# A state-space layer whose matrix multiplications run in the order of the program text, with rows normed in three groups

## The chip, the cores and the metric

The kernel runs on one core of one Trainium2 chip. The metric is device time in microseconds (us) of one execution; the median of the runs is given. One profiled execution supplies the trace from which all rows below are read. The engines are TensorE (PE, with its weight loads as PEld), VectorE (DVE), ScalarE (ACT), GpSimd (POOL) and SyncE (SP), whose queue issues most DMA transfers. An engine runs its own instructions strictly in order and waits on semaphores for what the others produce.

## The reference, cut to what matters

The program is one inference step of a small decoder: an S5 state-space layer, a shared K/V projection, and a stick-breaking attention layer. The change touches only the state-space layer, up to its gelu:

```python
h = _rms_norm(x, g_pre)                  # x * rsqrt(mean(x*x) + eps) * g
uz = h @ w_in                            # 1024 -> 2048
u, z = uz[..., :SSM_WIDTH], uz[..., SSM_WIDTH:]
y, hr, hi = _s5_scan(u, ...)             # 64 groups of 16 channels, 64 complex states each
y = jax.nn.gelu(y)
y = y * jax.nn.sigmoid(y @ w_glu + b_glu)
y = y * jax.nn.silu(z)
return x + _rms_norm(y @ w_out, g_post), hr, hi
```

There are 1024 prompt rows and 8 x 8 sample rows, all in float32. The scan is a linear recurrence with a complex factor for each group and state; `y` is a projection of the states plus `d_skip * u`.

## The kernel before, in words

**Norm.** The prompt is read as eight tiles of 128 rows (tile t has the positions t, t+8, t+16, ...), and a ninth tile has the 64 sample rows. For each tile the loop at L230 to L264 loads `xt`, takes the sum of squares on ScalarE (L240), the reciprocal root on GpSimd (`rstd`, L70: a pow and some tiny steps), multiplies the rows by it and by the norm weights `gpre` on VectorE in one instruction (L243), transposes in eight blocks on TensorE (L249) into the PSUM banks `psa` and `psb`, and splits the transposed block into a high part `xh` (ScalarE) and the rest `xl` (VectorE, helper L205). Five buffers hold `xt`.

**Input gemms.** `xh` and `xl` are kept as three groups of columns (`ACH`): 3, 3 and 2 row tiles of 136 columns (128 chunks of the prompt and 8 samples), so 408, 408 and 272 columns. One gemm makes 128 output channels of u or z: for each group of columns, a *chunk*, 24 matmuls (8 slices of 1024, times three products of the split parts, L147 to L149), a copy out by ScalarE, and after the third chunk a store to `u_d` or `zs_d`. There are eight u gemms and eight z gemms. Their weights are split into `whi` (ScalarE) and `wlo` (VectorE, and GpSimd for the odd z gemms).

**Scan.** A loop over eight feature tiles `ft` (8 groups of channels each). The *matrices* of a tile: VectorE makes `wb`, `ep`, `tm`, `fk`, `tn` from parameters; TensorE transposes `ep` (`psm`, L342) into `et` and multiplies `fk` with `wb` (L355) into `kp`, which SP's queue spreads into `tg`. The factors `cs` are made on GpSimd (six instructions with a scratch `m`; on VectorE for the first tile) and spread by four transfers into `cf` (L386). There is one `cs` buffer. Then three *units* of 3, 3 and 2 groups: `ug` (u read back from `u_d`) times `et` gives the chunk states `psb` (L403); ScalarE copies the halves crosswise into `tb`, VectorE multiplies `psb` by `cf`, GpSimd multiplies `tb`, VectorE adds, VectorE scans (L418); again ScalarE makes `ts`, GpSimd and VectorE multiply, and VectorE's sum is `hs`. TensorE turns `ug` times `tg` plus `hs` times `fk` into `psa` (L435, L436), ScalarE applies gelu into `gt` (L437), and after three units `gt` is stored to `y_d` (L439). Behind the loop the eight tiles of `y_d` are loaded and split into `yh` and `yl` (L455 to L457) for the GLU gemm, `psmm<-yh,whi_g`, which follows the last z gemm.

**Order.** A scheduler sets the order of each engine's instructions by simulated times and by priority: the matrices and the units stand in `tc.high_priority(OFA)`, so the gemms are laid matmul by matmul where it expects TensorE to be free.

Of the kernel before, what the change touches and what calls it, by code (L numbers as in the profile page):

```python
# [10 lines left out]
F32 = mybir.dt.float32  # L11
# [34 lines left out]
LAG = 3  # L46
SHARE = (0.1, 0.2, 0.3, 0.4)
# [22 lines left out]
def rstd(nc, pool, ss, out, n, mul, tag, eng=None):  # L70

    E = eng or nc.vector
    v = pool.tile([128, n], F32, name=f"v_{tag}", tag="rs_v")
    r0 = pool.tile([128, n], F32, name=f"r0_{tag}", tag="rs_r")
    h = pool.tile([128, n], F32, name=f"h_{tag}", tag="rs_h")
    e = pool.tile([128, n], F32, name=f"e_{tag}", tag="rs_e")
# [124 lines left out]
def s5_layer(tc, nc, io, wp, bank, cst, gains, ident, sgn, zs_d, u_d, y_d, s2):  # L201
# [5 lines left out]
    with ExitStack() as sx:  # L207
# [21 lines left out]
        for t in (8, 0, 1, 2, 3, 4, 5, 6, 7):  # L229
            n = 128 if t < 8 else NTS  # L230
            xt = start.tile([128, D], F32, name=f"xt{t}", tag="xt", bufs=5)
            nc.sync.dma_start(xt[:n], xp[t] if t < 8 else io["x_sample"])
            if t == 8:
                nc.sync.dma_start(gpre, io["a_gpre"].to_broadcast([128, D]))
                nc.sync.dma_start(cst, io["consts"][:, 0:129])
            sq = start.tile([128, D], F32, name=f"sq{t}", tag="sq")
            ss = par.tile([128, 1], F32, name=f"ss{t}", tag="ss", bufs=2)
            if n < 128:
                V.memset(ss, 1024.0)
            nc.scalar.activation(sq[:n], xt[:n], AF.Square, accum_out=ss[:n])  # L240
            rt = par.tile([128, 1], F32, name=f"rt{t}", tag="rt", bufs=2)
            rstd(nc, par, ss, rt, 1, 1.0 / D, f"a{t}", Q)
            V.scalar_tensor_tensor(xt[:n], xt[:n], rt[:n], gpre[:n], op0=ALU.mult, op1=ALU.mult)  # L243
            for i in range(2):
                ps = bank("a" if i else "b")
                p3 = ps.rearrange("p (a b) -> p a b", a=4)[:, :, :n]
                for j in range(4):
                    k = 4 * i + j
                    nc.tensor.transpose(p3[:, j], xt[:n, k * 128 : (k + 1) * 128], ident[:n, :n])  # L249
                ks = slice(4 * i, 4 * i + 4)  # L250
                for c, (t0, m) in enumerate(ACH):
                    if t < 8:
# [24 lines left out]
        def gemm_u(ft, w=None):
            nc.sync.dma_start(u_d[ft], gemm("u", ft, lambda o, ps: nc.scalar.activation(o, ps, AF.Copy), w))  # L278

        def gemm_z(ft):  # L280
            nc.sync.dma_start(zs_d[ft], gemm("z", ft, lambda o, ps: nc.scalar.activation(o, ps, AF.Copy)))

        gemm_u(0, w_first)
        gemm_u(1)
# [21 lines left out]
        for i in range(2):  # L306
# [8 lines left out]
        units = 0  # L315

        for ft in range(KT):
            with tc.high_priority(OFA):
                gs = slice(ft * 8, ft * 8 + 8)

                pk = pk_all[:, gs, :]
                sb = tp.tile([128, 4, 8, GC], F32, name=f"sb{ft}", tag="sb", bufs=2)
                nc.scalar.dma_start(sb, io["s5_bc"][ft, :, 0:4])
                wb = tp.tile([128, 4, 8, GC], F32, name=f"wb{ft}", tag="wb")
                tt(V, wb[:, 0:2], sb[:, 0:2], bc(bc(wri[:, 0, gs], 2, GC), 1, 2), ALU.mult)
                tt(V, wb[:, 2:4], sb[:, 0:2][:, ::-1], bc(wri[:, 1:3, gs], 3, GC), ALU.mult)
                tt(V, wb[:, 0:2], wb[:, 0:2], wb[:, 2:4], ALU.add)
                V.tensor_scalar(sb[:, 2:4], sb[:, 2:4], sgn, None, op0=ALU.mult)

                ep = tp.tile([128, 8, L, GC], F32, name=f"ep{ft}", tag="ep")  # L330
                tm = tp.tile([128, 8, L, GC], F32, name=f"tm{ft}", tag="tm")
                lrv = pk[:, :, K_LR : K_LR + 8][:, :, ::-1]
                liv = pk[:, :, K_LI : K_LI + 8][:, :, ::-1]
                tt(V, ep, bc(lrv, 3, GC), bc(wb[:, 0], 2, L), ALU.mult)
                tt(V, tm, bc(liv, 3, GC), bc(wb[:, 1], 2, L), ALU.mult)
                tt(V, ep, ep, tm, ALU.subtract)
                et = tp.tile([128, 8, 128], F32, name=f"et{ft}", tag="et", bufs=2)
                for i in range(2):
                    ps = bank("m")
                    for j in range(4):  # L340
                        g = 4 * i + j
                        nc.tensor.transpose(ps[:, j * 128 : (j + 1) * 128], ep[:, g].rearrange("p a b -> p (a b)"), ident)  # L342
                    nc.scalar.activation(et[:, 4 * i : 4 * i + 4, :], ps.rearrange("p (a b) -> p a b", a=4), AF.Copy)
                fk = tp.tile([128, 8, L + 1, GC], F32, name=f"fk{ft}", tag="fk", bufs=2)
                tm2 = tp.tile([128, 8, L + 1, GC], F32, name=f"tn{ft}", tag="tm")
                tt(V, fk, bc(pk[:, :, K_LR : K_LR + 9], 3, GC), bc(sb[:, 2], 2, L + 1), ALU.mult)
                tt(V, tm2, bc(pk[:, :, K_LI : K_LI + 9], 3, GC), bc(sb[:, 3], 2, L + 1), ALU.mult)
                tt(V, fk, fk, tm2, ALU.subtract)
                tg = tgs[ft % 2]
                kp = tp.tile([16, 8, 128], F32, name=f"kp{ft}", tag="kp")  # L350
# [1049 lines left out]
```

## Time and profile before

| | |
|---|---|
| median of 3 runs | 1499.05 us (1498.17 to 1500.22) |
| profiled execution | 1500.17 us |
| span of its trace | 1498.4 us |
| TensorE busy | 1415.8 us (94%) |
| VectorE busy | 935.0 us (62%) |
| ScalarE busy | 718.2 us (48%) |
| GpSimd busy | 493.7 us (33%) |

Busy times are sums over the whole span; the state-space layer is its first 340 us. The profiled execution is 1.8 us longer than its span.

### The profile page before, as it was taken

What the parts mean: (1) busy time and instruction counts of PE and PEld (TensorE: products, weight loads), DVE (VectorE), ACT (ScalarE), POOL (GpSimd) and SP (SyncE); (2) the same over time, 40 slices, a digit from 0 to 9 for tenths busy, and PEclk for the clock granted to TensorE, in tenths of its full rate; (3) what the DMA queues carried; (4) which work ended last, traced back from release to release, by engine and by line L of the source; (5) the groups of instructions that cost most, each with busy time, mean ns of one, the idle gap of its engine ahead of it and who ended that gap; (6) DMA issues with size and microseconds to landing.
All of it is one profiled execution on the core that took longest, in us unless ns stands there. A gap on an engine that the chain in (4) does not pass through costs nothing.

```text
span 1498.4 us, 26819 instructions
## 1 busy us (share of the span) xinstructions
PE 1415.8 (94%) x9648; PEld 1145.8 (76%) x9648; DVE 935.0 (62%) x1506; ACT 718.2 (48%) x1424; POOL 493.7 (33%) x473
## 2 busy tenths in 40 slices
PE   4987988899999989999999999999998999998997
PEld 3987978899977889999988877666565665565766
DVE  6877887758755531110122149897888888789545
ACT  5233454454434433332333347676665766576321
POOL 6556565325412132222111012433323233334200
PEclk9999999999999999999999999999999999999999
DMA  5345556674134252232288755979878686754026
GB/s 197 103 129 139 140 126 163 145 251 145 58 106 132 91 224 91 85 123 100 103 314 298 255 201 192 339 284 326 295 257 289 250 308 219 268 190 139 11 82 213
DMA packets 129670, 276.41 MB, mean 184 GB/s; under 512 B 21633, under 2 KB 66562, under 8 KB 129538
## 3 DMA queue, kind: packets, MB, share of 16 engines
q1 hardware_dynamic: 127234, 268.41, 54.0%
q10 hardware_dynamic: 2304, 6.29, 1.3%
q8 instruction: 76, 1.25, 0.3%
q14 instruction: 56, 0.46, 0.1%
HBM read 224.55 MB, written 39.35 MB: 176 GB/s over the span
## 4 chain that ended last, share of the span: by engine, by line
PE 75%; DVE 9%; POOL 5%; DMA 4%; issue 3%; ACT 2%; SPq 1%; DVEq 0%; POOLq 0%; ACTq 0%
PE psmm L147 7%; PE psmm L149 7%; PE psmm L148 7%; PE psqk L147 6%; PE psqk L148 6%; PE psqk L149 6%; PE psa L949 5%; PE psb L1182 5%; PE psb L1164 4%; PE psa L990 4%; PE psqk L1139 3%; PE psqk L1140 2%; DMA cf<-cs 2%; PE psa L147 2%; PE psa L149 2%
## 5 line engine op out<-in xcount | busy, mean ns | idle before, releaser
L1120 POOL TENSOR_TENSOR ql<-q,qh 128x256 fp32r<-128x256 f32 x64 | 62.5, 977 | 285.6 <-ACT qh L1119 246.5
L1141 ACT ACTIVATE F<-psqk,bp 128x384 f32<-128x384 f32 (+2 forms) x192 | 111.3, 580 | 64.6 <-PE psqk L1140 49.2
L1146 DVE TENSOR_TENSOR_SCAN F<-F,maskb 128x256 f32<-128x256 f32 (+3 forms) x128 | 131.2, 1030 | 14.0 <-ACT F L1141 13.6
L1149 POOL TENSOR_TENSOR S<-S,F 128x255 f32<-128x255 f32 (+3 forms) x64 | 100.8, 1574 | 115.7 <-DVE F L1148 22.5
L1142 ACT ACTIVATE S<-psqk,bp 128x384 f32<-128x384 f32 (+2 forms) x192 | 111.4, 583 | 22.7 <-PE psb L1164 22.6
L1164 PE MATMUL psb<-cst,S 128*128 128x128 f32 x576 | 96.7, 285 | 4.4 <-DVE og L1186 3.8
L1164 PEld LDWEIGHTS psb<-cst,S 128*128 128x128 f32 x576 | 67.3, 143 | 35.1 <-issue 20.5
L1148 DVE TENSOR_TENSOR_SCAN F<-F 128x384 f32<-128x384 f32 (+1 forms) x64 | 78.9, 1233 | 20.4 <-ACT F L1141 19.8
L1182 PE MATMUL psb<-at,vr 128*64 128x256 f32 (+1 forms) x640 | 90.0, 369 | 1.2 <-DVE at L1168 1.2
L949 PE MATMUL psa<-vp,sat 128*32 128x256 f32 x1024 | 86.1, 388 | 0.1
L1139 PE MATMUL psqk<-ks,qh 128*128 128x384 f32 (+2 forms) x192 | 77.4, 404 | 6.9 <-DVE ks L1104 5.2
L990 PE MATMUL psa<-kp,qbd 128*32 128x256 f32 x1024 | 75.5, 389 | 0.5 <-PE psb L1164 0.5
L1182 PEld LDWEIGHTS psb<-at,vr 128*64 128x64 f32 x640 | 46.7, 137 | 36.6 <-issue 10.3
L1168 DVE TENSOR_TENSOR at<-psb,maskb 128x384 f32<-128x384 f32 (+3 forms) x128 | 60.3, 478 | 21.3 <-PE psb L1164 20.7
L147 PE MATMUL psmm<-xh,whi_u 128*128 128x408 f32 (+1 forms) x192 | 65.3, 341 | 3.7 <-ACT ut L278 3.1
L147 PE MATMUL psmm<-x,whi_g 128*128 128x408 f32 (+1 forms) x192 | 66.6, 347 | 1.1 <-DVE gt L739 1.1
L943 DVE TENSOR_TENSOR_SCAN sF<-sF 128x513 f32<-128x513 f32 x32 | 44.4, 1388 | 36.1 <-ACT sF L940 35.8
L1139 PEld LDWEIGHTS psqk<-ks,qh 128*128 128x128 f32 x192 | 37.0, 193 | 37.8 <-ACT S L1142 12.8
L1140 PE MATMUL psqk<-ks,ql 128*128 128x384 f32 (+2 forms) x192 | 65.8, 344 | 0.0
L148 PE MATMUL psmm<-xl,whi_u 128*128 128x408 f32 (+1 forms) x192 | 65.4, 341 | 0.0
L149 PE MATMUL psmm<-x,wlo_g 128*128 128x408 f32 (+1 forms) x192 | 64.9, 338 | 0.2 <-DVE wlo_g L141 0.2
L148 PE MATMUL psmm<-x,whi_g 128*128 128x408 f32 (+1 forms) x192 | 65.1, 339 | 0.0
(452 smaller groups left out, 4234.6 us busy)
## 6 DMA issues: line engine op xcount, KB each, us to landing
kp<-cache_kT SPq DMA_DIRECT2D x128, 512.0 KB, 6.0
vp<-cache_v SPq DMA_DIRECT2D x128, 512.0 KB, 5.7
cf<-cs SPq DMA_DIRECT2D x32, 256.0 KB, 5.4
q<-q_d SPq DMA_DIRECT2D x128, 64.0 KB, 4.6
u_d<-ut SPq DMA_DIRECT2D x8, 544.0 KB, 2.8
ug<-u_d SPq DMA_DIRECT2D x64, 68.0 KB, 2.9
y_d<-gt SPq DMA_DIRECT2D x64, 68.0 KB, 2.4
zs_d<-zt SPq DMA_DIRECT2D x8, 544.0 KB, 4.5
```

The lines of the kernel that those rows point to most:

```text
L147: nc.tensor.matmul(ps, sh, mh, start=(k == 0), stop=False)
L148: nc.tensor.matmul(ps, sh, ml, start=False, stop=False)
L149: nc.tensor.matmul(ps, sl, mh, start=False, stop=(k == n - 1))
L949: self.nc.tensor.matmul(po[32 * r : 32 * r + 32, 0:256], a[:, 32 * r : 32 * r + 32], rhs[:, r * 256 : (r + 1) * 256], start=start, stop=stop)
L990: nc.tensor.matmul(ps[32 * r : 32 * r + 32, half * 256 : half * 256 + 256], self.qbd[:, 2 * r + e, s, :], kt[:, :, 2 * r + e, :], start=(e ...
L1139: nc.tensor.matmul(ps[:, :m], qh[:, w], ks[:, c0 : c0 + m], start=True, stop=False)
L1141: nc.scalar.activation(F[:, c0 : c0 + m], ps[:, :m], AF.Sigmoid, bias=bp[:, 1, h : h + 1], scale=-0.125)
L1142: nc.scalar.activation(S[:, c0 : c0 + m], ps[:, :m], AF.Sigmoid, bias=bp[:, 0, h : h + 1], scale=0.125)
L1146: V.tensor_tensor_scan(fr, fr, self.maskb[:, 512 - m : 512][:, ::-1], 1.0, ALU.mult, ALU.max)
L1149: (Q if i % 2 else V).tensor_tensor(S[:, 0 : n - 1], S[:, 0 : n - 1], F[:, 1:n], op=ALU.mult)
L1164: nc.tensor.transpose(ps[:, j * 128 : (j + 1) * 128], S[:, (j0 + j) * 128 : (j0 + j + 1) * 128], self.ident)
L1182: nc.tensor.matmul(po[hs, o:256], self.vr[pi][:, j, hs], ats[hh][j // 4][:, j % 4, o:256], start=(j == 0), stop=(j == nj - 1))
```

## The change

1. The norm runs over three groups of row tiles (four, three and two). All nine `xt` have a buffer. The multiplication by `gpre` is a GpSimd instruction of its own, ahead of the reciprocal root; the root is computed for a whole group, with its tiny steps on VectorE (the pow stays on GpSimd), and VectorE then multiplies each tile by its column of `rt`.
2. From behind the norm until the scan's pools are closed, TensorE's order is that of the program text (`tc.manual_schedule`). The gemms become a generator, `fills`, that yields after each chunk; the text takes six chunks, then seven and one around the first tile's matrices, then one in each of 26 steps of the scan loop (one more for each of the first three tiles). Five are left behind the loop.
3. The outputs of a unit come two units later than its states (`ULAG`), with three `hs` tiles instead of two. `tb` and `ts` share three buffers instead of four.

The other engines are still ordered by the scheduler.

```diff
+ULAG = 2
+FILLS = "u1 u2 z0 u3 u4 z1 u5 z2 u6 z3 u7 z4 z5 z6 z7".split()
...
-        for t in (8, 0, 1, 2, 3, 4, 5, 6, 7):
-            xt = start.tile([128, D], F32, name=f"xt{t}", tag="xt", bufs=5)
...
-            rstd(nc, par, ss, rt, 1, 1.0 / D, f"a{t}", Q)
-            V.scalar_tensor_tensor(xt[:n], xt[:n], rt[:n], gpre[:n], op0=ALU.mult, op1=ALU.mult)
...
+        for group in ((8, 0, 1, 2), (3, 4, 5), (6, 7)):
...
+            for e, t in enumerate(group):
...
+                xt = start.tile([128, D], F32, name=f"xt{t}", tag="xt", bufs=9)
...
+                nc.scalar.activation(sq[:n], xt[:n], AF.Square, accum_out=ss[:n, e : e + 1])
+                tt(Q, xt[:n], xt[:n], gpre[:n], ALU.mult)
+            rstd(nc, start, ss, rt, len(group), 1.0 / D, f"a{group[0]}")
...
+            for e, t in enumerate(group):
...
+                V.tensor_scalar(xt[:n], xt[:n], rt[:n, e : e + 1], None, op0=ALU.mult)
...
-        gemm_u(0, w_first)
-        gemm_u(1)
+        fills = chain(gemm("u", 0, w_first), *(gemm(n[0], int(n[1])) for n in FILLS))
+        st.enter_context(tc.manual_schedule(engines={mybir.EngineType.PE}))
+
+        def fill(n):
+            for _ in range(n):
+                next(fills, None)
+
+        fill(6)
...
+        first = matrices(0)
+        fill(7)
+        ahead(first)
+        fill(1)
+        ahead(first)
+        nxt = None
+        for n in range(3 * KT + ULAG):
+            ft, j = divmod(n, 3)
+            if n < 3 * KT:
+                with tc.high_priority(OFA):
+                    states(ft, j)
+            if j == 1 and ft + 1 < KT:
+                nxt = matrices(ft + 1)
+            fill(1)
+            if n >= ULAG:
+                with tc.high_priority(OFA):
+                    outputs(*divmod(n - ULAG, 3))
+            if nxt and j:
+                if j == 2 and ft < 3:
+                    fill(1)
+                ahead(nxt)
+                nxt = nxt if j == 1 else None
...
-        for ft in range(5, 8):
-            gemm_z(ft)
+        for _ in fills:
+            pass
```

`matrices(ft)` has the old matrices in two parts, up to the transposes, and from `kp` to the loads of `ug`; `states` and `outputs` have the old unit up to `hs`, and from `psa` on; `ahead` runs the next part with high priority.

TensorE, around the first and second feature tile, before (in names a number behind the letters is the feature tile or buffer, as in `ep1`, `hs0`; the last number only keeps names apart):

```order
L148 MATMUL psmm66_1699<-xl2_94,whi_u5_1642 128x272
L149 MATMUL psmm66_1699<-xh2_91,wlo_u5_1643 128x272
L147 MATMUL psmm66_1699<-xh2_91,whi_u5_1642 128x272
L342 MATMUL psm38_1075<-cst_63,ep1_1063 128x128 x4
L403 MATMUL psb43_1220<-ug1_1210,et1_1068 128x136
L435 MATMUL psa32_976<-ug0_952,tg0_792 128x136
L436 MATMUL psa32_976<-hs0_788,fk0_823 128x136
```

The same engine now, at the second tile's transposes:

```order
L149 MATMUL psmm39_1121<-xh0_89,whi_u4_1116 128x408
L150 MATMUL psmm39_1121<-xl0_92,whi_u4_1116 128x408
L151 MATMUL psmm39_1121<-xh0_89,wlo_u4_1117 128x408
L354 MATMUL psm40_1160<-cst_63,ep1_1154 128x128 x4
L354 MATMUL psm41_1166<-cst_63,ep1_1154 128x128 x4
L416 MATMUL psb42_1177<-ug0_1034,et0_952 128x136 x2
L149 MATMUL psmm43_1197<-xh1_90,whi_u4_1116 128x408
```

Before, the outputs of tile 0 and the transposes of tile 1 cut into a chunk (`psmm66`); now both stand between whole chunks of 24 matmuls, and the chunk at tile 1's transposes is of `u4`, no longer of `u5`.

GpSimd at the first unit, before (`cs1` and `cs2` are the factors of tiles 1 and 2, `tb0_0` the first unit's copy, `ts0_0` its second):

```order
L205 TENSOR_TENSOR cs1_1111<-cs1_1111,m1_1112 128x512
L205 TENSOR_TENSOR m2_1370<-uu_569 128x512
L205 TENSOR_TENSOR tb0_0_966<-tb0_0_966,cf0_861 128x384
L205 TENSOR_TENSOR cs2_1369<-uu_569 128x512 x2
L205 TENSOR_TENSOR cs2_1369<-cs2_1369,m2_1370 128x512
L205 TENSOR_TENSOR ts0_0_977<-ts0_0_977,cf0_861 128x384
```

and now:

```order
L207 TENSOR_TENSOR cs1_1284<-cs1_1284,m1_1285 128x512
L207 TENSOR_TENSOR m2_1576<-uu_504 128x512
L207 TENSOR_TENSOR cs2_1575<-uu_504 128x512 x2
L207 TENSOR_TENSOR cs2_1575<-cs2_1575,m2_1576 128x512
L207 TENSOR_TENSOR m2_1576<-uu_504 128x512
L207 TENSOR_TENSOR dk1_1273<-cst_63,dcol_505 16x128
L207 TENSOR_TENSOR tb0_0_1047<-tb0_0_1047,cf0_1029 128x384
L207 TENSOR_TENSOR cs2_1575<-cs2_1575,m2_1576 128x512
L143 TENSOR_TENSOR wlo_z1_1331<-wraw_z1_1328,whi_z1_1330 128x1024
L207 TENSOR_TENSOR m3_1860<-uu_504 128x512
L207 TENSOR_TENSOR ts0_0_1057<-ts0_0_1057,cf0_1029 128x384
```

Most of `cs2` has moved ahead of the first unit's `tb0_0`, and a `wlo_z1` stands between `tb0_0` and `ts0_0`.

VectorE in the norm, now, at the third group (`rt6` is the group's root, `xl0` the first group of columns; `ex1_dt` and `ex3_dt` are parameter work):

```order
L254 TENSOR_SCALAR xt6_282<-xt6_282,rt6_280 128x1024
L254 TENSOR_SCALAR xt7_287<-xt7_287,rt6_280 128x1024
L102 SCALAR_TENSOR_TENSOR ex3_dt_519<-ex3_dt_519,ex2_dt_518 128x96
L207 TENSOR_TENSOR xl0_92<-psa8_198,xh0_89 128x4x128
L207 TENSOR_TENSOR xl1_93<-psb9_235,xh1_90 128x4x128
```

and before, at the same two tiles:

```order
L205 TENSOR_TENSOR xl1_93<-psb9_258,xh1_90 128x4x128
L205 TENSOR_TENSOR xl1_93<-psa10_265,xh1_90 128x4x128
L243 SCALAR_TENSOR_TENSOR xt6_336<-xt6_336,rt6_341,gpre_88 128x1024
L98 TENSOR_SCALAR ex3_dt_584<-ex2_dt_583 128x96
L102 TENSOR_SCALAR ex1_dt_582<-ex1_dt_582 128x96
L243 SCALAR_TENSOR_TENSOR xt7_368<-xt7_368,rt7_373,gpre_88 128x1024
L100 SCALAR_TENSOR_TENSOR ex3_dt_584<-ex3_dt_584,ex2_dt_583 128x96
```

Before, `xl1` of the fourth row tile was made ahead of the last tiles' multiplications; now the last block of `xl0`, of the third row tile, comes behind them.

## Rows read from the trace of the kernel before

**Rows 1.** Busy time (us, instructions) of engines by stretch; clock, DMA share, GB/s.

```profile
0.00:50.00 50.00, 27.03 (x146) 24.09 (x147) 34.13 (x82) 23.79 (x47) 24.35 (x74) 0.90 0.44 148
50.00:87.40 37.40, 35.92 (x218) 35.62 (x216) 33.54 (x85) 9.18 (x16) 25.54 (x26) 1.00 0.53 146
95.07:274.74 179.67, 152.39 (x1038) 144.25 (x1036) 140.87 (x231) 78.61 (x179) 109.61 (x85) 0.95 0.55 134
274.74:294.54 19.80, 18.53 (x136) 17.62 (x137) 14.52 (x33) 12.51 (x29) 5.43 (x6) 1.00 0.75 178
...
87.39:328.17 240.78, 212.23 (x1440) 203.11 (x1441) 176.24 (x298) 111.10 (x243) 129.00 (x101) 0.96 0.59 148
```

**Rows 2.** What TensorE waited for, 0 to 520 us: total, times, longest.

```profile
PE psb L249 <- DVE xt L243: 19.9, 5, 11.8
PE psa L435 <- ACT gt L437: 10.0, 4, 5.0
PE psa L436 <- DVE hs L205: 8.4, 4, 3.5
```

**Rows 3.** Timeline: start, duration, what, [idle before it <- releaser].

```profile
49.80 0.35 PE L147 MATMUL psmm<-xh,whi_u 128*128 128x408 f32 x1
...
87.39 0.66 PE L342 MATMUL psm<-cst,ep 128*128 128x128 f32 x4 [1.48 <-DVE ep L205]
...
95.07 0.57 DVE L205 TENSOR_TENSOR psb<-psb,cf 128x384 f32<-128x384 f32 x1 [2.07 <-ACT tb L411]
...
99.80 0.57 DVE L205 TENSOR_TENSOR psb<-psb,tb 128x384 f32<-128x384 f32 x1 [3.87 <-POOL tb L205]
...
274.74 0.57 DVE L205 TENSOR_TENSOR psb<-psb,cf 128x384 f32<-128x384 f32 x1 [0.58 <-ACT tb L411]
...
289.45 0.55 DVE L205 TENSOR_TENSOR hs<-psb,ts 128x381 f32<-128x381 f32 x1
...
294.54 0.57 DVE L205 TENSOR_TENSOR psb<-psb,cf 128x384 f32<-128x384 f32 x1 [0.29 <-ACT tb L411]
...
294.57 0.40 PE L435 MATMUL psa<-ug,tg 128*128 128x136 f32 x2
294.81 0.40 PE L436 MATMUL psa<-hs,fk 128*128 128x136 f32 x2
...
309.68 0.42 DVE L205 TENSOR_TENSOR hs<-psb,ts 128x254 f32<-128x254 f32 x1 [0.43 <-POOL ts L205]
...
328.17 0.35 PE L147 MATMUL psmm<-yh,whi_g 128*128 128x408 f32 x1
```

**Rows 4.** What VectorE waited for, 95.07 to 274.74 us.

```profile
DVE psb L205 <- ACT ts L426: 12.3, 13, 1.1
DVE psb L205 <- POOL tb L205: 8.0, 3, 3.9
DVE hs L205 <- POOL ts L205: 8.0, 5, 3.4
DVE psb L205 <- ACT tb L411: 6.8, 10, 2.1
DVE sb L328 <- DMA sb<-s_bc: 3.2, 2, 1.7
```

**Rows 5.** GpSimd by form, 0 to 340 us: busy us, mean ns | idle before.

```profile
L205 POOL TENSOR_TENSOR cs<-uu 128x512 f32<-128x512 f32 x14 | 19.3, 1396 | 26.7 <-DMA cf<-cs 24.1 <-DMA y_d<-gt 2.6
...
L141 POOL TENSOR_TENSOR wlo_z<-wraw_z,whi_z 128x1024 fp32r<-128x1024 f32 x4 | 9.5, 2368 | 2.6 <-ACT whi_z L140 2.6
L79 POOL TENSOR_TENSOR r_a<-v_a,e_a 128x1 f32<-128x1 f32 x9 | 7.9, 882 | 0.6
...
L127 POOL TENSOR_TENSOR cmb_g<-uu,sc 128x64 f32<-128x64 f32 x1 | 5.4, 5439 | 0.0
```

**Rows 6.** VectorE by form, the same stretch.

```profile
L243 DVE SCALAR_TENSOR_TENSOR xt<-xt,rt,gpre 128x1024 f32<-128x1024 f32 x8 | 10.7, 1333 | 2.7 <-POOL rt L83 2.6
...
L112 DVE TENSOR_SCALAR ra_a<-ra_a 128x288 f32<-128x288 f32 x1 | 0.3, 304 | 0.0
```

More of the change, by code (lines that the diff above doesn't have):

```diff
@@ L267, in gemm @@
+        def gemm(which, ft, w=None):
             wh, wl = w or weights(which, ft)
@@ L305, in s5_layer @@
         h_t = []
-        for i in range(2):
+        for i in range(ULAG + 1):
             hs = tp.tile([128, 3, W], F32, name=f"hs{i}")
@@ new lines, in states @@
+        def states(ft, j):
+            g0, n = ACH[j]
+            pk, et, fk, tg, cof, sif = made[ft]
+            ug = rows_in[ft]
+            pg = bank("b")
+            for i in range(n):
+                nc.tensor.matmul(pg[:, i * W : (i + 1) * W], et[:, g0 + i, :], ug[:, g0 + i, :], start=True, stop=True)
+            pg3 = pg[:, : n * W].rearrange("p (a b) -> p a b", a=n)
+            gsl = slice(ft * 8 + g0, ft * 8 + g0 + n)
+            gl = slice(g0, g0 + n)
+            ta = pg3[:, :, 0:NC]
+            tb = work.tile([128, 3, NC], F32, name=f"tb{ft}_{g0}", tag="tb", bufs=3)
+            nc.scalar.activation(tb[0:64, :n], pg3[64:128, :, 0:NC], AF.Copy)
+            nc.scalar.activation(tb[64:128, :n], pg3[0:64, :, 0:NC], AF.Copy, scale=-1.0)
+            tt(V, ta, ta, cof[:, gl], ALU.mult)
+            tt(V, sst[:, gsl, :], pg3[:, :, NC:W], pk[:, gl, K_LH : K_LH + NS], ALU.add)
+            tt(Q, tb[:, :n], tb[:, :n], sif[:, gl], ALU.mult)
+            tt(V, ta, ta, tb[:, :n], ALU.add)
+            for i in range(n):
+                g = ft * 8 + g0 + i
+                V.tensor_tensor_scan(
+                    ta[:, i], rho[:, g : g + 1].to_broadcast([128, NC]), ta[:, i], 0.0, ALU.mult, ALU.add
+                )
+            hs = h_t[(3 * ft + j) % (ULAG + 1)]
+            ts = work.tile([128, 3, NC], F32, name=f"ts{ft}_{g0}", tag="tb", bufs=3)
+            nc.scalar.activation(ts[0:64, :n], ta[64:128], AF.Copy, scale=-1.0)
+            nc.scalar.activation(ts[64:128, :n], ta[0:64], AF.Copy)
+            tt(Q, ts[:, :n], ts[:, :n], sif[:, gl], ALU.mult)
+            nc.scalar.activation(hs[:, :n, NC:W], pk[:, gl, K_H0 : K_H0 + NS], AF.Copy)
+            tt(V, ta, ta, cof[:, gl], ALU.mult)
+            tt(V, hs[:, :n, 1:NC], ta[:, :, 0 : NC - 1], ts[:, :n, 0 : NC - 1], ALU.add)
+            tt(V, l1[:, gsl], ta[:, :, NC - 1], ts[:, :n, NC - 1], ALU.add)
+            started[ft, j] = hs
@@ new lines, in outputs @@
+        def outputs(ft, j):
+            g0, n = ACH[j]
+            gl = slice(g0, g0 + n)
+            pk, et, fk, tg, cof, sif = made[ft]
+            ug, hs = rows_in[ft], started.pop((ft, j))
+            if j == 0:
+                rows_out[ft] = work.tile([128, 8, W], F32, name=f"gt{ft}", tag="gt")
+            gt = rows_out[ft]
+            py = bank("a")
+            for i in range(n):
+                g = g0 + i
+                o = py[:, i * W : (i + 1) * W]
+                nc.tensor.matmul(o, tg[:, g, :], ug[:, g, :], start=True, stop=False)
+                nc.tensor.matmul(o, fk[:, g, 1:, :].rearrange("p a b -> p (a b)"), hs[:, i, :], start=False, stop=True)
+            nc.scalar.activation(gt[:, gl], py[:, : n * W].rearrange("p (a b) -> p a b", a=n), AF.Gelu_apprx_tanh)
+            if j == len(ACH) - 1:
+                ydst = y_d[ft].rearrange("(g c) (t n) -> t c g n", c=GC, t=L)
@@ L438, in s5_layer, with ahead @@
                 for t in range(L):
                     nc.sync.dma_start(ydst[t], gt[t * GC : (t + 1) * GC])
-            if ft >= 3:
-                gemm_z(ft - 3)
+        def ahead(gen):
+            with tc.high_priority(OFA):
+                next(gen)
+        first = matrices(0)
[13 more added lines that the diff above has]
+            if n >= ULAG:
+                with tc.high_priority(OFA):
+                    outputs(*divmod(n - ULAG, 3))
[4 more added lines that the diff above has]
+                nxt = nxt if j == 1 else None
```

270 lines of the change are left out of this document (115 added, 155 removed).

## The prediction

> **What bounds the kernel now.** I first read each engine's busy time by stretch [rows 1], then TensorE's waits, then times of single instructions. The change touches only the state-space layer, whose last input gemm ends at 328.17 us [rows 3], where the GLU gemm begins. What follows is the same in both kernels, so the question is by how much 328.17 moves.
>
> Three stretches are limited differently. In 0 to 50 TensorE works 27.0 us [rows 1]; of its idle time 19.9 us is five waits for a normed row `xt` from VectorE [rows 2]. From 50 to 87.4 it is full: 35.92 us in 37.4, for 218 matmuls. Three input gemms of 72 matmuls make up 216 of them, so one gemm is 11.9 us; split by columns (408, 408, 272) a gemm's chunks are 4.45, 4.45 and 2.97 us. In the third, from 87.39 on, TensorE's waits are for the two ends of the scan chain, `gt` (10.0 us) and `hs` (8.4 us) [rows 2].
>
> That chain runs on VectorE. Its pace shows at the first `cf` multiplication of each feature tile: 95.07 for the first of the eight, 274.74 for the seventh, 294.54 for the eighth [rows 3]. Six periods take 179.67 us, 29.95 each. VectorE works 140.87 us of that [rows 1], 23.5 a period. Its idle time [rows 4] is 19.1 us for ScalarE's copies (12.3 + 6.8; each unit's chain has them, and no order removes them) and 19.2 us for GpSimd and the `sb` load (8.0 + 8.0 + 3.2). So a period is 23.5 work + 3.2 copies + 3.2 GpSimd and loads. TensorE could do the layer faster; VectorE's chain, with the gemms laid beside it, sets the end.
>
> **The norm.** Removed: nine VectorE multiplications of 1.33 us [rows 6], and 9 x 6 tiny GpSimd steps, of which a pow is 0.88 us [rows 5]. Added on VectorE: nine TENSOR_SCALAR; the 128x288 one takes 0.30 us, so one of 1024 columns costs at most 0.30 x 1024/288 = 1.08, and I take that. VectorE gains about 2 us, in a stretch where it isn't full. Added on GpSimd: nine two-operand multiplications of 1024 columns. No such one is in the trace; the nearest is `wlo_z` with the same shape, 2.37 us. At this price they take 21.3 us, and three pows 2.6 more. Lower bound: VectorE's own 1.33 us for the row's multiplication (12 us in all). Upper bound: the price when GpSimd is held up, below.
>
> When do they start? VectorE's first multiplication is followed by TensorE's first transposes, in front of which TensorE had been idle since the start; the row and the norm weights are there at about 8 us (an estimate from the longest `xt` wait, 11.8 us [rows 2], less the multiplication and some 2 us of tiny steps). The last pow therefore ends at about 8 + 21.3 + 2.6 = 32 us, or 36 with the waits for squares in between. In VectorE's new order the two rows of the third group stand ahead of one `xl` that the second half of the first chunk needs; 36 + 3 us (tiny steps, two TENSOR_SCALAR, the `xl`) = 39, and then TensorE has 2.2 + 4.45 + 2.97 = 9.6 us left of the first gemm: 49, and 51.5 with transposes between, against 49.80 now [rows 3]. I take 51.5: 1.7 us late, between 2 us early and 8 late.
>
> **The start of the loop.** By the old order the transposes of `ep` come after twelve chunks, at 87.39. By the new one they come after thirteen (six, then seven), and one more chunk goes between them and `kp`. From 51.5 ten chunks are 39.9 us: transposes at 91.4 to 92, `kp` and the first states some 7 us later. The first `cf` multiplication moves from 95.07 to about 102.4. What waits there is VectorE's chain alone; TensorE does gemm work in that time that it need not do later.
>
> GpSimd's new order has all six operations on `cs` of tile 1 and most of those of tile 2 ahead of the first `tb` multiplication. The `cs` of tile 2 must wait until `cs` of tile 1 has left by its four `cf` transfers; such waits of GpSimd are 24.1 us in all [rows 5]. So the first unit's sum comes at about 112 us rather than 99.80 [rows 3], while VectorE can do the next tile's matrices; I cost it inside the pace.
>
> **The pace of the loop.** VectorE's work and the ScalarE copies in a tile don't change: 23.5 + 3.2 = 26.7 us, the lower bound. The upper bound is the present 29.95. Three `hs` tiles instead of two and TensorE two units behind take away waits of TensorE, not of VectorE. `tb` and `ts` share three buffers instead of four: the copies for a unit then wait for the `hs` of the unit two before, which VectorE has done a unit's time earlier, so I cost it at nothing. VectorE's own waits, for GpSimd, could go where the new order lets `tb` and `ts` pass the `cs` work; mostly it doesn't, and SP's queue, which issues `tg`, `cf`, `ug`, `y_d` and the z weights in one row, is as full as before. In the other direction a unit's state matmuls now wait for a whole chunk, up to 4.45 us; with three PSUM buffers VectorE has then still two units at hand. I take 28.0, two fifths of the 3.2 us remaining, nearer to the lower end since the largest single waits, 3.9 and 3.4 us [rows 4], sit at the first tiles, where VectorE now has the next matrices to do. The last period has no matrices ahead; now 19.8 us with 14.5 of work [rows 1], I take 15.3 (15 to 19.8). So the eighth tile's `cf` multiplication, call its time X, falls at 102.4 + 6 x 28.0 + 15.3 = 285.7, where it is 294.54 now; bounds 277.6 and 301.9.
>
> **What TensorE has left after X.** This is where the text's order costs. Now the gemms end 328.17 - 294.54 = 33.6 us after X. In the new order five chunks remain behind the loop (4.45 + 2.97 + 11.9 = 19.3), and one stands between each two of the last units. The `hs` of the seventh tile's middle unit starts about 5 us before X (289.45 against 294.54 [rows 3]). From there TensorE has its outputs and those of the four units after, 13 groups of an L435 and an L436, each 0.24 us (they start so far apart [rows 3]) = 6.1; five state matmuls of the same width, 1.2; four chunks in the loop, 4.45 + 4.45 + 2.97 + 4.45 = 16.3; and 19.3 behind it: 42.9, so X + 38. The later `hs` bind less: the last one comes 15.1 after X (309.68 [rows 3]) and has 0.9 + 19.3 behind it, X + 35.3. So break-even is X = 290, and my X gives 324: 4.2 us earlier. `yl` of the last tile, which the GLU gemm needs last, follows the last output through a store, a load and a split as now, and may hold that gemm up; I give 0.5 us to it.
>
> **Sum.** -3.7 us on the profiled execution, whose own time is 1500.17 (span 1498.4 and 2 outside): 1496.5. It is 1.1 above the median of the runs, so the forecast is 1495.5.
>
> **The rivals.**
> *VectorE's waits stay (slower).* GpSimd keeps `cs` between `tb` and `ts`, and `cf` lands as late as now. At 29.95 a period, and 19.8 for the last, X is 301.9 and the end 340: 1511. From X above 293 on it is slower by 0.2%; with a period of 29 X is 293.5 to 296, 1503 to 1505. For it: the `cs` wait of 24.1 us [rows 5], and the first `tb` that now stands behind it. Against it: late units can be hidden behind matrices.
> *GpSimd is held up in the head (slower or none).* A `cmb_g` of 64 columns took 5.44 us, where one on `cs` with 512 columns takes 1.40 [rows 5]; something held it up, and VectorE was busy beside it. If each of the nine multiplications loses one VectorE instruction of about 1 us, the third group's pow comes at 45, the first gemm ends near 60 and everything is 8 us later, less the 4 of the forecast: 1503.
> The Trainium skill ("SBUF — State Buffer", section on the two separate sides) says that a GpSimd operation and a VectorE operation with two SBUF inputs shut each other out of a shared port pair for the whole instruction. By that rule the multiplications would each wait out one VectorE instruction, which is this rival; the 5.44 us row agrees, the 2.37 of `wlo_z` hardly shows it.
> *The waits for GpSimd go (much faster).* With 26.7 a period X is 277.6 and the end 316; with the head on time as well 312: 1483 to 1488. TensorE's own work is no bound there: 212 us less the chunk, from 92 on, would end before 300 [rows 1].
> *The order does nothing.* X near 290: what is saved in the loop is spent at the end. 1499.
>
> **How the numbers follow.** Forecast case (X of 283 to 291, -7 to +1 us, 1493 to 1500) 0.44; waits stay 0.25; waits go 0.19; held up in the head 0.07; nothing 0.05. A difference under 0.2% (3 us) is what a measurement of this kernel can't tell from none. Faster: 0.28 of the forecast case + 0.19 + 0.01 = 0.48. Same: 0.16 + 0.05 + 0.01 = 0.22. Slower: 0.24 + 0.06 = 0.30. The range of 8 in 10 goes from within the fast rival, 1482, to within the slow one, 1508; the forecast case alone holds 1493 to 1500.
>
> **What would show it.** In the new profile: first gemm ending at 51.5, first `cf` multiplication at 102, the eighth at 286, last gemm ending 38 us after it. TensorE's waits in the loop should not vanish but gather in front of the outputs (`hs`). I am wrong if the interval between `cf` multiplications stays at 30 or falls under 27, or if TensorE's first gemm is over 5 us late.

## The result: 1.7% slower, and where the time went

The changed kernel takes 1525.59 us in the median of four runs, the kernel before 1499.12; the ratio is 1.0174 (95% interval 1.0156 to 1.0191). The forecast was 1495.5, with 1508 as the upper end of its range. It was wrong in sign and size.

The profiled execution took 1522.92 us, with a span of 1521.1. TensorE does as much work as before (1410.9 us, before 1415.8); it only stands idle longer. The stretches of the changed kernel that answer to [rows 1], up to the end of the input gemms:

```profile
0.00:50.00 50.00, 13.02 (x61) 10.92 (x61) 35.69 (x64) 20.23 (x38) 26.75 (x26) 1.00 0.41 147
50.00:105.86 55.86, 52.99 (x324) 52.32 (x325) 45.75 (x123) 15.43 (x28) 30.02 (x30) 1.00 0.39 117
117.07:289.14 172.07, 138.94 (x955) 134.28 (x954) 134.32 (x227) 75.10 (x173) 104.86 (x81) 0.93 0.52 133
289.14:307.92 18.78, 14.66 (x103) 13.81 (x102) 13.00 (x30) 10.09 (x24) 5.43 (x6) 0.91 0.56 119
307.92:351.20 43.28, 43.28 (x283) 43.26 (x283) 20.32 (x35) 19.98 (x35) 10.40 (x8) 1.00 0.67 209
```

In the first 50 us TensorE works 13.0 us instead of 27.0. The last row has no idle time at all: from the eighth tile's `cf` multiplication (307.92) to the GLU gemm (351.20) TensorE is full, for 43.28 us. What it waited for, as in [rows 2]:

```profile
PE psb L260 <- DVE xt L254: 30.9, 3, 28.4
PE psm L354 <- ACT et L355: 29.7, 8, 8.1
PE psb L260 <- DVE xl L207: 3.8, 1, 3.8
PE psa L459 <- DVE hs L207: 3.6, 3, 2.1
```

The waits at the outputs have gone from 18.4 us to 3.6. In their place stand 28.4 us before the first transpose, and a wait that the old list did not show so: in front of the second four transposes of each tile, until ScalarE has copied the first four out of the one `psm` bank. The timeline at the points of [rows 3]:

```profile
28.43 0.69 PE L260 MATMUL psb<-cst,xt 64*128 64x64 f32 x4 [28.43 <-DVE xt L254]
...
65.32 0.35 PE L149 MATMUL psmm<-xh,whi_u 128*128 128x408 f32 x1
...
105.86 0.60 PE L354 MATMUL psm<-cst,ep 128*128 128x128 f32 x4
...
117.07 0.55 DVE L207 TENSOR_TENSOR psb<-psb,cf 128x384 f32<-128x384 f32 x1
...
289.14 0.57 DVE L207 TENSOR_TENSOR psb<-psb,cf 128x384 f32<-128x384 f32 x1 [0.57 <-ACT tb L424]
...
307.92 0.56 DVE L207 TENSOR_TENSOR psb<-psb,cf 128x384 f32<-128x384 f32 x1 [0.57 <-ACT tb L424]
...
351.20 0.35 PE L149 MATMUL psmm<-yh,whi_g 128*128 128x408 f32 x1
```

The second gemm starts at 65.32 us (before 49.80), and the layer's end moves by 351.20 - 328.17 = 23.0 us, which is the whole difference of the two spans (22.7). It splits at the `cf` multiplications of tiles 1, 7 and 8:

| | before | after | moved | forecast |
|---|---|---|---|---|
| start to first `cf` multiplication | 95.07 | 117.07 | +22.0 | +7.3 |
| six periods | 179.67 | 172.07 | -7.6 | -11.7 |
| last period | 19.80 | 18.78 | -1.0 | -4.5 |
| from there to the GLU gemm | 33.63 | 43.28 | +9.7 | +4.4 |
| sum | 328.17 | 351.20 | +23.0 | -4.5 |

Of the 27.5 us between forecast and result, 14.7 are the start, 7.6 the pace and 5.3 the end.

Why the start is late stands in VectorE's and GpSimd's timelines of the changed kernel. First VectorE:

```profile
14.85 2.36 DVE L80 TENSOR_SCALAR v_a<-ss 128x4 f32<-128x4 f32 x1 [3.96 <-ACT sq L246]
18.39 1.12 DVE L80 TENSOR_SCALAR v_a<-ss 128x3 f32<-128x3 f32 x1 [1.19 <-ACT sq L246]
20.50 2.29 DVE L82 TENSOR_TENSOR h_a<-r_a 128x4 f32<-128x4 f32 x1 [0.99 <-POOL r_a L81]
22.83 2.26 DVE L83 TENSOR_TENSOR h_a<-h_a,v_a 128x4 f32<-128x4 f32 x1
25.12 2.27 DVE L84 TENSOR_SCALAR h_a<-h_a 128x4 f32<-128x4 f32 x1
27.43 0.16 DVE L85 TENSOR_TENSOR rt<-r_a,h_a 128x4 f32<-128x4 f32 x1
```

and GpSimd beside it:

```profile
19.44 1.03 POOL L81 TENSOR_TENSOR r_a<-v_a,e_a 128x4 f32<-128x4 f32 x1
20.42 6.95 POOL L207 TENSOR_TENSOR xt<-xt,gpre 128x1024 f32<-128x1024 f32 x3
27.31 1.11 POOL L81 TENSOR_TENSOR r_a<-v_a,e_a 128x3 f32<-128x3 f32 x1
```

An instruction on four columns takes 0.16 us at 27.43, but 2.3 us while GpSimd's multiplications run, which is the length of one of them (6.95 / 3 = 2.32). The three chained steps on `h_a` come out one per multiplication, and the first step, `v_a` at 14.85, took as long beside an earlier one. The step at 27.43 came after the last of the three multiplications, while GpSimd was in a pow (27.31), and was not held up.

### The profile page after: what moved, and what is told of

It is laid out like the page before. It is cut to its first block, busy times and chain, and to the rows that moved or that the text cites. A ratio compares the mean times of both kernels' runs of the same rounds, so it can differ in the third digit from the quotient of the medians.

```text
span 1521.1 us, 26795 instructions
## 1 busy us (share of the span) xinstructions
PE 1410.9 (93%) x9648; PEld 1145.5 (75%) x9648; DVE 932.3 (61%) x1524; ACT 717.1 (47%) x1424; POOL 495.4 (33%) x425
## 4 chain that ended last, share of the span: by engine, by line
PE 70%; DVE 9%; DMA 3%; issue 2%; POOL 2%; ACT 2%; SPq 1%; DVEq 0%; POOLq 0%; ACTq 0%
PE psmm L149 6%; PE psmm L151 6%; PE psmm L150 6%; PE psqk L150 6%; PE psqk L149 6%; PE psqk L151 6%; PE psa L999 4%; PE psb L1232 4%; PE psa L1040 4%; PE psb L1214 4%; PE psqk L1189 2%; PE psa L149 2%; PE psa L151 2%; PE psa L150 2%; PE psqk L1190 2%
## 5 line engine op out<-in xcount | busy, mean ns | idle before, releaser
L1192 ACT ACTIVATE S<-psqk,bp 128x384 f32<-128x384 f32 (+2 forms) x192 | 111.3, 582 | 22.7 <-PE psb L1214 22.7
L1214 PE MATMUL psb<-cst,S 128*128 128x128 f32 x576 | 95.7, 283 | 4.9 <-DVE og L1236 3.8
L1218 DVE TENSOR_TENSOR at<-psb,maskb 128x384 f32<-128x384 f32 (+3 forms) x128 | 60.3, 478 | 21.0 <-PE psb L1214 20.3
L149 PE MATMUL psmm<-xh,whi_z 128*128 128x408 f32 (+1 forms) x192 | 66.1, 344 | 2.0 <-ACT ut L284 2.0
L149 PE MATMUL psmm<-x,whi_g 128*128 128x408 f32 (+1 forms) x192 | 66.6, 347 | 1.1 <-DVE gt L789 1.1
L150 PE MATMUL psmm<-xl,whi_u 128*128 128x408 f32 (+1 forms) x192 | 65.3, 340 | 1.8 <-DVE xl L207 1.8
L1189 PEld LDWEIGHTS psqk<-ks,qh 128*128 128x128 f32 x192 | 36.9, 192 | 37.4 <-ACT S L1192 12.4
```

Of the source, the lines that this page charges most:

```text
L149: nc.tensor.matmul(ps, sh, mh, start=(k == 0), stop=False)
L150: nc.tensor.matmul(ps, sh, ml, start=False, stop=False)
L1189: nc.tensor.matmul(ps[:, :m], qh[:, w], ks[:, c0 : c0 + m], start=True, stop=False)
L1192: nc.scalar.activation(S[:, c0 : c0 + m], ps[:, :m], AF.Sigmoid, bias=bp[:, 0, h : h + 1], scale=0.125)
L1214: nc.tensor.transpose(ps[:, j * 128 : (j + 1) * 128], S[:, (j0 + j) * 128 : (j0 + j + 1) * 128], self.ident)
```

## Experiments

Times are medians; ratios are to the kernel before, measured beside each. To compare the kernels one by one, this table has for each, from its trace, the start of the last copy-out of the first gemm, the first state sum (`sst`) of tiles 1 and 8, the mean of the seven periods between, the start of the GLU gemm, and the time from tile 8's `sst` to it. In tiles 1 and 8 `sst` stands 0.6 to 4.7 us behind the tile's first `cf` multiplication (4.7 in two_banks' tile 1), so a difference of half a microsecond between two periods says little.

| kernel | us | first gemm | tile 1 | tile 8 | period | GLU | rest |
|---|---|---|---|---|---|---|---|
| before | 1499.1 | 50.8 | 95.7 | 295.1 | 28.5 | 328.2 | 33.0 |
| changed | 1525.6 | 65.6 | 118.7 | 308.8 | 27.2 | 351.2 | 42.4 |
| norm_only | 1516.2 | 66.7 | 107.7 | 305.9 | 28.3 | 346.1 | 40.2 |
| order_only | 1509.5 | 50.3 | 103.7 | 293.3 | 27.1 | 335.7 | 42.4 |
| gpre_dve | 1515.2 | 50.9 | 107.6 | 298.9 | 27.3 | 341.2 | 42.4 |
| gpre_halves | 1525.0 | 63.6 | 122.3 | 313.4 | 27.3 | 355.7 | 42.4 |
| et_gap | 1527.5 | 66.6 | 118.4 | 310.8 | 27.5 | 354.9 | 44.1 |
| two_banks | 1541.4 | 78.5 | 134.2 | 324.4 | 27.2 | 370.2 | 45.9 |
| late_banks_changed | 1529.9 | 66.5 | 118.7 | 311.1 | 27.5 | 357.0 | 45.9 |
| early_fills | 1514.0 | 49.8 | 103.5 | 302.3 | 28.4 | 332.8 | 30.5 |
| early_start | 1504.1 | 49.9 | 102.1 | 291.9 | 27.1 | 327.7 | 35.8 |
| early_two_banks | 1507.4 | 60.0 | 111.3 | 292.0 | 25.8 | 330.7 | 38.7 |
| late_banks | 1504.6 | 49.8 | 101.7 | 290.9 | 27.0 | 328.4 | 37.4 |
| sp_raw | 1506.7 | 51.4 | 103.5 | 292.2 | 27.0 | 328.0 | 35.8 |
| less_chain | 1506.7 | 49.6 | 104.6 | 286.3 | 26.0 | 332.2 | 45.9 |
| both_off | 1491.0 | 50.3 | 102.3 | 277.7 | 25.1 | 315.9 | 38.1 |

**One half of the change at a time.** norm_only is the old kernel with the new norm, order_only the changed one with the old norm.

> The new norm with the old loop and the old (scheduler's) order of TensorE. Theory 1: while GpSimd multiplies rows by the norm weights, VectorE's tiny steps on 128x4 take 2.3 us each, so the first transposes come at 28 us and the first gemm ends at about 65 rather than 50; nothing later makes up for it: 1511 to 1516. Rival: VectorE's chain in the loop sets the end and the late head is absorbed: 1499 to 1502.

> The old norm with the new loop, TensorE in the order of the text. Theory 2: TensorE stops in front of the second four transposes of each tile until ScalarE has copied out the first four (one psm bank), some 30 us in all, of which about 10 are a loss against the old waits in the loop: 1506 to 1512, first gemm ending at 50. Rival: the order alone is a gain as forecast, and all the loss is the head's: 1494 to 1499. Second rival: all the loss is the order's: 1522 to 1526.

norm_only: ratio 1.0112 (1.0091 to 1.0133); order_only: 1.0072 (1.0047 to 1.0097). The parts cost 16.5 and 9.9 us and add up to the whole (26.4 of 26.5). The late head is not absorbed, and the order alone is a loss too: its periods are 1.4 us shorter, but the first tile comes 8.0 us later and 9.4 us more are left behind the eighth.

**The norm weights back on VectorE (gpre_dve).**

```diff
-                tt(Q, xt[:n], xt[:n], gpre[:n], ALU.mult)
...
-                V.tensor_scalar(xt[:n], xt[:n], rt[:n, e : e + 1], None, op0=ALU.mult)
+                V.scalar_tensor_tensor(xt[:n], xt[:n], rt[:n, e : e + 1], gpre[:n], op0=ALU.mult, op1=ALU.mult)
```

> The changed kernel with the norm weights multiplied on VectorE again, in one instruction with the root; three groups and the text's order stay. Theory 1: VectorE's 128x4 steps fall from 2.3 to about 0.2 us, first transposes at 17 to 19, first gemm ends at 50 to 53, and the time falls by 10 to 14: 1511 to 1515. Rival (the grouping itself, not GpSimd, makes the head late): 1522 to 1526.

1515.2, ratio 1.0095 (1.0078 to 1.0112), 10.4 us under the changed kernel. VectorE's same steps:

```profile
14.93 0.17 DVE L80 TENSOR_SCALAR v_a<-ss 128x4 f32<-128x4 f32 x1 [4.31 <-ACT sq L246]
16.31 0.16 DVE L82 TENSOR_TENSOR h_a<-r_a 128x4 f32<-128x4 f32 x1 [1.21 <-POOL r_a L81]
16.51 0.16 DVE L83 TENSOR_TENSOR h_a<-h_a,v_a 128x4 f32<-128x4 f32 x1
16.71 0.17 DVE L84 TENSOR_SCALAR h_a<-h_a 128x4 f32<-128x4 f32 x1
```

They take 0.16 us, the first transposes come at 18.44 and the first gemm ends on time. GpSimd's pow comes earlier too, since no multiplications stand ahead of it in GpSimd's own queue (19.44 in the changed kernel):

```profile
15.25 1.03 POOL L81 TENSOR_TENSOR r_a<-v_a,e_a 128x4 f32<-128x4 f32 x1 [13.85 <-DVE v_a L80]
```

So of the 10.5 us by which the first rows are taken up later in the changed kernel (27.63 against 17.11), 4.2 are the pow behind the multiplications and 6.3 the held-up steps. Some 6 us against order_only remain; 3.9 of them lie between the first gemm and the first tile (107.6 against 103.7), and the rest behind the sixth tile. They were not taken apart.

**The same work in shorter instructions (gpre_halves).**

```diff
-                tt(Q, xt[:n], xt[:n], gpre[:n], ALU.mult)
+                for c in range(2):
+                    hf = slice(512 * c, 512 * c + 512)
+                    tt(Q, xt[:n, hf], xt[:n, hf], gpre[:n, hf], ALU.mult)
```

> The changed kernel with each of GpSimd's nine multiplications cut into two of 512 columns; its work stays the same. Theory 1a: a VectorE instruction waits out the GpSimd instruction that is under way, so VectorE's 128x4 steps fall from 2.3 us to about 1.2, the first transposes come at 23 to 25 us, and the kernel is 3 to 6 us faster than the changed one: 1519 to 1523. Rival (the two engines share a rate while GpSimd is busy, whatever the length of its instructions): the steps stay at 2.3 us, 1524 to 1527.

1525.0, no gain. The mechanism is as theory 1a has it:

```profile
20.96 1.22 DVE L82 TENSOR_TENSOR h_a<-r_a 128x4 f32<-128x4 f32 x1 [2.22 <-POOL r_a L81]
22.21 1.19 DVE L83 TENSOR_TENSOR h_a<-h_a,v_a 128x4 f32<-128x4 f32 x1
23.43 1.19 DVE L84 TENSOR_SCALAR h_a<-h_a 128x4 f32<-128x4 f32 x1
24.66 1.18 DVE L85 TENSOR_TENSOR rt<-r_a,h_a 128x4 f32<-128x4 f32 x1
25.76 1.33 DVE L1264 TENSOR_SCALAR aim<-pr,cst 128x64 f32<-128x64 f32 x1
```

A VectorE instruction waits out one GpSimd instruction, whatever that one's length (4.94 us for four halves, 1.24 each). But the scheduler put parameter steps (`aim`) ahead of the rows, and each of those waits as well; the first transposes come at 29.1. What the four steps won, the parameter steps lost.

**A chunk between the halves of the transposes (et_gap).**

```diff
+                if i == 0:
+                    yield
...
             fill(1)
+            if nxt and j == 2:
+                ahead(nxt)
```

> The changed kernel with one chunk of a gemm between the two halves of each tile's transposes. Theory 2: the 29.7 us of TensorE's waits for et go down to under 8, and the end comes 12 to 22 us earlier: 1503 to 1513. Rival: VectorE's chain sets the end, so the waits only move to the outputs (hs): 1520 to 1526.

1527.5, ratio 1.0184 (1.0165 to 1.0202): the rival's, 1.5 us above its range. The waits for `et` fall to 14.9 us, and others come for them (of TensorE, 60 to 330 us):

```profile
PE psb L418 <- DMA ug<-u_d: 11.2, 4, 5.6
PE psm L354 <- ACT et L355: 11.0, 3, 6.6
PE psa L461 <- DVE hs L207: 10.6, 3, 3.8
PE psm L370 <- ACT et L355: 3.9, 1, 3.9
```

**More chunks before the end (early_fills, early_start).** Both have the old norm.

```diff
-                if j == 2 and ft < 3:
+                if j == 2:
```

> The old norm and the text's order (1509.5), with the extra chunk in the scan loop for all tiles, not only the first three: one chunk is left behind the loop instead of five. Theory 2a: what counts is the work that the text leaves TensorE after the eighth tile's first states; four chunks (some 15 us) move into TensorE's waits of the loop, so the end comes 8 to 15 us earlier: 1495 to 1502. Rival (the chunks delay the states, so VectorE's chain comes later by as much): 1507 to 1512.

> As early_fills, and the loop starts after twelve chunks, as in the kernel before, rather than fourteen. Theory 2b: VectorE's chain starts some 8 us earlier, the two chunks go into TensorE's waits of the loop, and what is left behind the loop is three chunks: 1490 to 1496, faster than the kernel before. Rival (the start is VectorE's: its parameters or the cf transfers are not there earlier): as early_fills, within 2 us.

early_fills: 1514.0, ratio 1.0099 (1.0081 to 1.0116), no faster than order_only (the intervals overlap). What is left behind the eighth tile falls by 12 us, but that tile comes 9 us later (302.3), and its `y` with it: the GLU gemm starts at 332.8 and then stops for `yh`:

```profile
PE psmm L149 <- ACT yh L499: 5.8, 3, 2.3
PE psmm L149 <- ACT gs L532: 1.4, 1, 1.4
PE psmm L150 <- DVE yl L500: 1.1, 2, 0.6
```

early_start, which besides takes `fill(6)` for `fill(7)` and no chunk between transposes and `kp`, takes 1504.1, ratio 1.0030 (1.0019 to 1.0041): 5.4 us better than order_only, 4.3 us behind the kernel before. Neither theory's numbers: TensorE reached the first transposes at 86.2 instead of 90.9, but stood 4.79 us for `et` there, and tile 1 comes 1.6 us earlier, not 8.

**A second bank for the transposes.** TensorE's order stays; `psm` has two banks, `psa` one.

```diff
-        banks({"mm": 2, "a": 2, "b": 3, "m": 1})
+        banks({"mm": 2, "a": 1, "b": 3, "m": 2})
```

> The changed kernel with two PSUM banks for the transposes (psm) and one for the outputs (psa), TensorE's order as it is. Theory 3: the 29.7 us of TensorE's waits for et are only where it waits for VectorE's chain; with two banks they move to psb and psa (hs), the chain's pace stays at 27 us a tile and the time within 4 us of the changed kernel: 1521 to 1528. Rival (the waits are a loss of their own): 10 to 20 us faster, 1505 to 1515.

> early_start (1504.1) with the same two banks. Theory 3: within 3 us of early_start, 1501 to 1507. Rival: 8 to 15 us faster, 1489 to 1496, which would beat the kernel before.

1541.4 (ratio 1.0274) and 1507.4 (1.0059): inconclusive, since the norm's transposes use `psa` too and the first gemm ended 10 to 13 us late. late_banks (on early_start) and late_banks_changed switch the banks behind `fill(6)` instead.

> early_start (1504.1) with the second psm bank and the single psa bank only from the loop on, so that the norm's transposes keep two psa banks. Two banks from the start ended the first gemm 10 us late, and from the first transposes of ep to the GLU gemm took 233.6 us instead of 241.5. Theory 4 (TensorE's waits for et were a loss of their own, hidden by the later head): 6 to 10 us faster than early_start, 1494 to 1498, a little faster than the kernel before. Rival (VectorE's chain sets the end, theory 3; the shorter stretch only came from the later head): 1501 to 1507.

> The changed kernel with the same late banks. Theory 4: 5 to 12 us faster than the changed kernel, 1513 to 1520, the waits for et gone. Theory 3: 1522 to 1528, the waits at hs, ug and psb instead.

1504.6, ratio 1.0025 (1.0014 to 1.0037), and 1529.9, ratio 1.0204 (1.0187 to 1.0221): no gain. In late_banks the eight waits for `et` between the halves of the transposes are gone; one of 4.2 us stands in front of `kp` (L362) instead, and TensorE's longest waits are now (60 to 330 us):

```profile
PE psa L453 <- DVE hs L207: 8.6, 4, 5.4
PE psb L410 <- DMA ug<-u_d: 6.9, 2, 3.7
PE psb L410 <- DVE psb L425: 4.3, 1, 4.3
PE psm L362 <- ACT et L349: 4.2, 1, 4.2
PE psb L410 <- DVE psb L207: 3.2, 1, 3.2
```

**Less work in VectorE's chain (less_chain, on order_only).**

```diff
-            tt(V, tm2, bc(pk[:, :, K_LI : K_LI + 9], 3, GC), bc(sb[:, 3], 2, L + 1), ALU.mult)
-            tt(V, fk, fk, tm2, ALU.subtract)
```

> order_only (1509.5) without two of VectorE's matrix operations of each tile (the second product of fk and its subtraction, 1.73 + 1.54 us), so that fk lacks its imaginary part; TensorE's instructions and their order are the same. Theory 3 (VectorE's chain sets the end): 23 us less work over seven periods; periods of 24 to 25 us instead of 27, the eighth tile's first states 12 to 20 us earlier and the end as well: 1490 to 1498. Rival (TensorE's own order sets the pace, by the wait for et or by its chunks): 1505 to 1510.

1506.7, ratio 1.0048 (1.0032 to 1.0063). Between the two: the period falls by 1.1 us where 3.8 us of work went (1.65 + 2.12 in order_only; the expectation had the kernel before's 3.3), and the GLU gemm starts 3.5 us earlier. The median falls by 2.8 us, which is within the spread of the runs. TensorE's waits for `et` shrink from 26.8 to 20.3 us, and others come that order_only did not have (60 to 330 us):

```profile
PE psm L347 <- ACT et L348: 20.3, 8, 8.4
PE psb L406 <- DMA ug<-u_d: 10.7, 5, 3.4
```

TensorE passes the eighth tile's transposes 8.1 us earlier than in order_only (271.85 against 279.92) and then stops for 3.45 us in front of that tile's states, for `ug` (282.83); from there to the GLU gemm it has no pause. VectorE's chain is not the limit by itself, and theory 3 does not hold as I had it.

**Both together, and ScalarE's queue.** both_off is late_banks without the two operations; sp_raw is early_start with `nc.sync.dma_start(wraw, ...)` for all weights.

> late_banks (1504.6) without the two operations of less_chain, so that fk lacks its imaginary part. Theory 5 (two limits of nearly the same length: TensorE stopping at the transposes, and VectorE's chain; each hides the other): periods of 23 to 25 us, 1486 to 1496. Rival (a third limit, such as the transfers of ug and cf or ScalarE's queue): 1500 to 1505.

> early_start (1504.1) with the u weights loaded by SP's queue like the z weights, so that ScalarE's queue holds no transfer that waits for a buffer. Theory 6 (ScalarE's queue, held up by such waits, delays et, tb and ts): 4 to 10 us faster, 1494 to 1500, TensorE's waits for et from 28 to under 20 us. Rival (ScalarE waits for VectorE's scans anyway): 1502 to 1507.

both_off: 1491.0, ratio 0.9951 (0.9938 to 0.9965). Like less_chain it leaves out part of `fk`, so it is no candidate. The second bank gave nothing, the shorter chain 3 us (on order_only), both 13.6 us against late_banks. These times flatter the pair, since less_chain lost part of its gain to that last stop. The periods are the fairer measure: the bank alone takes off 0.1 us, the two operations alone 1.1, both 2.0 (27.1 to 25.1). That fits two limits of nearly the same length that hide each other; it is not a full proof, because early_start without the two operations was not run. TensorE's longest waits in both_off (60 to 330 us) are again for a transfer:

```profile
PE psb L407 <- DMA ug<-u_d: 9.2, 3, 3.6
```

sp_raw: 1506.7, ratio 1.0049 (1.0034 to 1.0064), the waits for `et` at 28.2 us as before: the weight loads in ScalarE's queue are not what holds `et` up. ScalarE itself waits 69.9 us there for VectorE's scans.

No version that computes the reference beat the kernel before; early_start and late_banks come nearest.

## Why the prediction was wrong

**The norm: the step that failed.** "VectorE gains about 2 us" took VectorE's instructions at their durations on a quiet chip, and the rival that I wrote down, "GpSimd is held up in the head", had the right contact between the two engines with the loser on the wrong side. GpSimd's multiplications took 2.33 to 2.36 us, as the 2.37 that I gave them, and only the last two were held up (2.45 and 2.79); VectorE's steps were, at 2.3 us each. The third group's pow came as forecast, at 37 us where I had 36. What failed is the step behind it, "36 + 3 us (tiny steps, two TENSOR_SCALAR, the `xl`) = 39":

```profile
35.56 1.70 POOL L81 TENSOR_TENSOR r_a<-v_a,e_a 128x2 f32<-128x2 f32 x1 [1.18 <-DVE v_a L80]
...
48.06 1.41 DVE L254 TENSOR_SCALAR xt<-xt,rt 128x1024 f32<-128x1024 f32 x2
```

The third group's rows are done at 49.5, ten microseconds late. VectorE could not multiply its first rows before 27.63, so their splits and the parameter work stood in its queue ahead of the third group; the forecast followed GpSimd's queue only. The first gemm ended at 65.3 and not 51.5, which is one of the signs of being wrong that the prediction names, and norm_only puts the price of the whole norm at 16.5 us; in the changed kernel, 10.4 us go with the multiplications' move to GpSimd (gpre_dve). The Trainium skill ("SBUF — State Buffer", section on the two separate sides) says that a VectorE instruction that has two SBUF inputs or runs in a two-port mode shares a port pair with GpSimd, and that whichever of the two starts first has the pair for its whole instruction. The trace agrees: in a row of GpSimd instructions VectorE got in only between two of them. I had read the rule for one direction alone, since the `cmb_g` row [rows 5] showed GpSimd as the loser.

**The start of the loop.** Two more chunks ahead of the loop moved the first `cf` multiplication by 7.1 us in order_only (95.07 to 102.12), whose first gemm is on time. The forecast's 7.3 held 1.7 for the norm, so 5.6 stand against 7.1: the term was a little small. In the changed kernel the late first gemm came on top.

**The pace.** Forecast 28.0 a period and 15.3 for the last; measured 28.7 and 18.8 [172.07 / 6, and the last stretch]. The direction was right, at two thirds of the forecast gain in the six periods and a fifth in the last. The mechanism was not, so that 28.7 lies near 28.0 is in part luck. I took VectorE's work as unchanged and the gain from its waits for GpSimd. What it waited for in the six periods, as in [rows 4]:

```profile
DVE psb L207 <- ACT ts L437: 12.8, 13, 1.1
DVE hs L207 <- POOL ts L207: 8.4, 6, 3.0
DVE psb L207 <- POOL tb L207: 7.4, 4, 4.6
DVE psb L207 <- ACT tb L424: 4.4, 12, 0.6
```

The waits for GpSimd stayed, 15.8 us where there were 16.0. It is VectorE's busy time that fell, from 140.9 to 134.3 us (227 instructions instead of 231), and its waits for ScalarE's copies, from 19.1 to 17.2. Why the busy time fell was not taken apart.

"Three `hs` tiles ... take away waits of TensorE, not of VectorE" held: the waits for `hs` went. What I did not see is the single `psm` bank. By the old order chunks lay between the two halves of the transposes; by the text they follow each other, and eight waits, 29.7 us, came in. Taking them away alone gained nothing (et_gap, late_banks).

**What TensorE has left.** "X + 38" was X + 43.3. I looked for the binding `hs` among the last five units only. The binding point was earlier: in the changed kernel TensorE is without a pause from the second half of tile 8's transposes (295.38 us, behind a wait of 3.90) to the GLU gemm, 55.8 us; in order_only from 279.92 to 335.73, 55.8 us again. With the text's order this remainder is fixed. The change of order therefore gains only if X comes 9.7 us earlier, and it came 2.1 earlier in order_only (292.46).

**The rivals.** The slower one that I held likeliest, "VectorE's waits stay", had its condition right and its price wrong: the waits stayed, and yet a period took 28.7 and not 29.95 us. What made the kernel slower was the head, which that rival did not name, and the remainder behind X. The rival that named the head had half its size, with the first gemm ending near 60 us.

**What stays open.** both_off and less_chain suggest that no single engine sets 27 us a period in the text's order; which handovers do is not shown, and the waits for `ug` that come in both are a third suspect. The 6 us between gpre_dve and order_only, which are the grouped norm's without GpSimd's multiplications, were not taken apart.

## What to carry to other kernels

Moving an operation to GpSimd is not paid by GpSimd alone: price it by the short, chained VectorE instructions beside it, each of which can cost a whole GpSimd instruction, and by what then stands behind it in GpSimd's own queue. Before writing TensorE's order by hand, look for buffers of one (here a PSUM bank) between two groups that the hand order puts side by side, and sum up what stands behind the last stop, from each stop and not only from the last results. Where a removed wait comes back elsewhere at the same length, take two suspects away together before you call either harmless.

## What the runs showed of the hardware

A VectorE instruction on 128x4 took 2.26 to 2.36 us beside GpSimd multiplications of 2.32 us, 1.18 to 1.22 beside ones of 1.24, and 0.16 to 0.17 with none (gpre_dve) or beside a pow (27.43). Four transposes behind a wait of 8.10 us (130.43) took 1.11 us at a granted clock of 0.50, the lower of its two levels (1.2 GHz), where those at 105.86 took 0.60 at 1.00 (2.4 GHz); from 117 to 289 us the granted clock was 0.93 of full, in the kernel before 0.95 from 95 to 275.
